# State-space heads: wrong-order token pairs zeroed by GpSimd behind the exponential, instead of masks added on TensorE

## The chip, the cores and the metric

The kernel runs on one core of one Trainium2 chip. The metric is the device time of one execution in microseconds (us). The kernel before takes 971.55 us, the median of three runs (970.40 to 972.12). One more execution was taken with the hardware profiler; it took 970.61 us, of which 968.5 us lie between the core's first and last instruction (the span).

The engines are named as in the profile: PE is TensorE's matmul side and PEld its weight load, DVE is VectorE, ACT is ScalarE, POOL is GpSimd, SP is the queue that issues the DMAs.

## The reference, cut to what matters

The program is one step of a small two-layer backbone. Layer 0 mixes by Fourier and attention, layer 1 by two recurrences side by side, one of them a bidirectional state-space model with 16 heads. Every layer is followed by a SwiGLU FFN. There are 128 context tokens and 256 latent tokens, worked on as three chunks of 128. The change is in the state-space heads, inside a chunk:

```
acs    = cumsum(dt * A)                        # per head and direction
diff   = acs[q] - acs[k]                       # 128 x 128 pairs of tokens
causal = tril(ones(Q, Q))                      # only k not after q
decay  = exp(where(causal, diff, -inf))        # wrong order: 0
y_diag = sum_k (C[q].B[k]) * decay[q,k] * dt[k] * x[k]
```

The backward direction does the same on the flipped sequence, so there the pairs on the other side of the diagonal count.

## The kernel before, in words

All activations lie with channels on the 128 partitions and tokens along the free dimension (384 tokens, or 386 columns with two extra columns for the modulation's shift). Every projection multiplies fp32 weights as a high and a low fp32r part: three matmuls of 386 columns for each 128x128 block of weights (`mm3`). The weights come in as chunks of eight blocks (`wr`); ACT writes the high part (`wh`) and DVE the low part (`wl`) of each chunk. These two steps run through the whole program and feed PE.

`Kernel.record` writes all operations into a recorder, and `Recorder.schedule` then sets the order of every engine's instructions by a list scheduler with a fixed cost for each operation: at each step it takes the operation that can start first by its costs. Within an engine the instructions then run strictly in that order. A changed operation or cost can therefore move any instruction behind it.

`odd_mixer` is layer 1's mixer. Its input projection yields 27 tiles; as each leaves PE, its own work on ACT and DVE follows: convolutions and SiLU (`cv`, `ct`), gates and scans of the RG-LRU (`lru`, `lru_scan`), and for every second `xs` tile two calls of `ssd`, each for two heads. So there are four groups of four heads. For each head `ssd` (line 1408) does the following:

- It builds `diff + log dt` for both directions in PSUM. One matmul `own x mv` (128x128 by 128x384) adds row and column terms; `own` and `mv` hold 112 used rows of 128, picked by the selector table `selv`.
- A second matmul into the same bank, `identr x mask` (line 1424), adds -2^100 to each pair in the wrong order. `mask` is made once in `deltas` from two triangular constants by two DVE instructions; `identr` is a rounded identity that ACT writes at the program's start.
- ACT takes the exponential out of PSUM into a tile `M` (128x384), one for each direction.
- DVE adds the two `M` tiles and multiplies by `cb` (the products C.B of the group).
- PE multiplies `M` with the tokens `xt`, together with the part of the carried state (`exs x Hc`), and DVE makes `ysum` of it.

POOL does nothing in this program but small memsets.

Of the kernel before, what the change touches and what calls it, by code (L numbers as in the profile page):

```python
# [101 lines left out]
def selectors():  # L102

    s = np.zeros((18, 128, NC_), np.float32)
    for h in range(16):
        for c in range(3):
            s[h, [c * 16 + h, 64 + c * 16 + h], c * 128:(c + 1) * 128] = 1.0
    for d in range(2):  # L110
        s[16 + d, [48 + d, 50 + d], 0:128] = 1.0
    return s


# [76 lines left out]
def R(v):  # L191
    return v.resolve() if isinstance(v, Vw) else v
# [279 lines left out]
class Kernel:  # L472
# [112 lines left out]
    def memset(self, out, v, eng="POOL"):  # L585
# [3 lines left out]
        else:  # L589
            self.rec.add("POOL", 0.1 + out.free / 900, [out], [], lambda: nc.gpsimd.memset(R(out), v))  # L590

    def dma(self, out, in_):
        nc = self.nc
        v = out if isinstance(out, Vw) else in_
        self.rec.add("SP", v.shape[0] * v.free * 4 / 400e3, [out], [in_], lambda: nc.sync.dma_start(R(out), R(in_)))  # L595
# [208 lines left out]
    def even_mixer(self):  # L804
# [216 lines left out]
        def pre(k):  # L1021
            if k == KC:
                return

            for j in ((0, 2) if k == 0 else (k + 2,) if k % 2 == 0 else ()):
                if j < KC:
                    if j:
                        self.ensure(-(-6 * j // NBLK), 0)
                    self.ada_pe(0, CM, j, 2)
                    self.gains(0, "norm_mix", j, j + 2)  # L1030
                    self.dma(self.x[:, j:j + 2, :], self.io["x"][:, j:j + 2, :])
                    self.ada_pe(0, SM, j, 2)
                    for i in (j, j + 1):
                        self.norm_xg(i)
                        self.shifts(0, SM, i)
                        self.norm_sq(i)
                    if j == 6:
                        self.dma(self.cons[:, NC00:NC0], self.io["consts"][:, NC00:NC0])
                        self.norm_close()
            if k == 6:  # L1040
                held.append(self.rec.ops[-1])
            if k == 7:
                self.early = self.EARLY
                self.rec.gate = held[0]
                load_consts("cos", "sin")
                pairs()
                self.rec.gate = None
            if k == 0:
                self.act(self.identr, self.ident, AF.Copy)

        self.dma(self.cons[:, CO["ident"]], self.io["consts"][:, CO["ident"]])
        self.norm_open()
# [69 lines left out]
    def odd_mixer(self):  # L1122
# [116 lines left out]
        def deltas(p):  # L1239

            t = self.slot("dtT")
            self.evac(t, p)
            for i in range(2):
                self.ts(t[:, SEG[i]], t[:, SEG[i]], t[:, 128 + i:129 + i], ALU.add)
            q = self.bank()
            for c in range(3):
                self.tp(q[:, c * 128:(c + 1) * 128], t[:, CH[c]:CH[c] + 128])
            v = self.tile("dv", 96, F32, "c")
            self.tt(v.split(3), q[:, 0:384].split(3)[:, :, 0:32], self.sm("dt_bias").unsqueeze(1).to_broadcast([128, 3, 32]), ALU.add)
            dt = self.tile("dt", 96, F32, "c")  # L1250
            self.softplus(dt, v, 96)
            dta = self.tile("dta", 96, F32, "c")
            d3 = dta.split(3)
            self.tt(d3, dt.split(3), negA.unsqueeze(1).to_broadcast([128, 3, 32]))
            q = self.bank()
            for c in range(3):
                self.mm(q[:, c * 32:c * 32 + 16], self.con("lo"), dta[:, c * 32:c * 32 + 16])
                self.mm(q[:, c * 32 + 16:c * 32 + 32], self.con("up"), dta[:, c * 32 + 16:c * 32 + 32])
            tot = self.bank()
            self.mm(tot[:, 0:96], self.ones, dta)  # L1260
            acs = self.tile("acs", 96, F32, "c")
            self.act(acs, q[:, 0:96], AF.Copy)
            de = self.tile("de", 96, F32, "c")
            self.tt(de, tot[:, 0:96], acs, ALU.subtract)
            self.act(de, de, AF.Exp)
            et = self.tile("et", 96, F32, "c")
            self.act(et, tot[:, 0:96], AF.Exp)
            q = self.bank()
            for c in range(3):
                self.tp(q[0:32, c * 128:(c + 1) * 128], acs[:, c * 32:(c + 1) * 32])  # L1270

            rr = self.slot("rr", NC_, F32R)
            self.act(rr[0:32], q[0:32, :NC_], AF.Copy)
            self.tt(rr[32:64], q[0:32, :NC_], rr[0:32].bitcast(F32), ALU.subtract)
            er = self.slot("er", NC_)
            self.act(er[0:32], q[0:32, :NC_], AF.Exp)
            ee = self.slot("ee", NC_, F32R)
            self.memset(ee[64:128].bitcast(F32), 0.0)
            self.split_hl(ee[0:32], ee[32:64], er[0:32])

            nacs = self.tile("nacs", 96, F32, "c")
            self.ts(nacs, dt, 2.0 ** -126, ALU.max)
            self.act(nacs, nacs, AF.Ln)
            steps = self.tile("steps", 96, F32, "c")
            q = self.bank()
            own = []
            for d in range(2):
                v = steps[:, d * 48:d * 48 + 48]
                ds = slice(d * 16, d * 16 + 16)
                self.tt(v.split(3), nacs.split(3)[:, :, ds], acs.split(3)[:, :, ds], ALU.subtract)  # L1290
                self.tp(q[0:48, d * 128:(d + 1) * 128], v)

                w, t = self.slot("ownt", 128), self.slot("own", 128, F32R)
                self.dma(w, self.io["selv"][16 + d, :, 0:128])
                self.act(t, w, AF.Copy)
                self.act(t[0:48], q[0:48, d * 128:(d + 1) * 128], AF.Copy)
                self.tt(t[64:112], q[0:48, d * 128:(d + 1) * 128], t[0:48].bitcast(F32), ALU.subtract)
                own.append(t)
            pick = self.slot("pick", 32)
            for z in range(2):  # L1300
                zs = slice(32 * z, 32 * z + 32)
                self.act(pick[zs], self.ident[zs, zs], AF.Copy)

            sel = [self.tile("sel", 1024, F32R, "k") for _ in range(2)]
            for z in range(2):
                self.memset(sel[z][64:128].bitcast(F32), 0.0)
                for d in range(2):
                    self.act(sel[z][0:64].split(8)[:, :, d * 64:d * 64 + 64],
                             pick[0:64, d * 16 + z * 8:d * 16 + z * 8 + 8].unsqueeze(2).to_broadcast([64, 8, 64]), AF.Copy)

            mask = []
            for mk in ("lo", "up"):
                t = self.slot("mask", NC_, F32R)
                self.ts(t.split(3), self.con(mk).unsqueeze(1).to_broadcast([128, 3, 128]), 2.0 ** 100, ALU.mult, -(2.0 ** 100), ALU.add)
                mask.append(t)
            dd = self.tile("dd", 96, F32, "c")
            self.tt(dd, dt, de)
            S.update(dd=dd, own=own, et=et, rr=rr, ee=ee, sel=sel, mask=mask)

        def bc(i, p):  # L1320
            y = conv(p, self.sm("csw")[:, (8 + i) * 4:(8 + i) * 4 + 4], self.sm("csb")[:, 8 + i:9 + i])
# [86 lines left out]
        def ssd(j):  # L1408
# [4 lines left out]
            for hb in range(2):  # L1413
                h = 2 * j + hb
                q = [self.bank() for _ in range(2)]

                t, mv = self.slot("mvt", NC_), self.slot("mv", NC_, F32R)
                self.dma(t, self.io["selv"][h])
                self.dma(t[48:52], S["rr"].bitcast(F32)[h:64:16])
                self.act(mv, t, AF.Copy)  # L1420
                for d in range(2):
                    self.mm(q[d][:, :NC_], S["own"][d], mv, True, False)
                for d in range(2):
                    self.mm(q[d][:, :NC_], self.identr, S["mask"][d], False, True)
                    m = self.slot("M", NC_)
                    self.act(m, q[d][:, :NC_], AF.Exp)
                    M[hb, d] = m
                self.tt(M[hb, 0], M[hb, 0], M[hb, 1], ALU.add)
                self.tt(M[hb, 0], M[hb, 0], S["cb"][g])
                q = self.bank()  # L1430
                self.mm(q[:, 0:256], S["sel"][h // 8][:, h % 8 * 128:h % 8 * 128 + 128], S["ee"][:, 128:384])
                ex[hb] = self.slot("exs", NS_)
                self.tt(ex[hb], q[:, 0:256], S["cs"][g])
# [113 lines left out]
    def record(self, n_chunks):  # L1547
# [8 lines left out]
        self.memset(self.scT, 0.0)  # L1556
        self.mod = [Tl(f"mod{l}", None, (128, 48, 2), F32).view() for l in range(2)]
        self.G = Tl("G", None, (128, KC, 2), F32).view()
        self.identr = self.tile("identr", 128, F32R)
        self.ident = self.con("ident")  # L1560
        self.ones = self.con("ones")
        self.act(self.scT[:, :, 0:2], self.sm("condT").split(8), AF.Silu)
# [166 lines left out]
```

## Time and profile before

| what | value |
|---|---|
| median of three runs | 971.55 us |
| profiled execution, and its span | 970.61 us, 968.5 us |
| PE busy | 946.1 us, 98% of the span |
| DVE busy | 730.9 us, 75% |
| ACT busy | 498.1 us, 51% |
| POOL busy | 6.5 us, 1% |
| granted TensorE clock, mean | 0.998 |

Matmuls are pipelined and the profile models their ends, so PE's busy share says that it had work and not that it ran at its peak; how long a matmul occupies PE is read from the distance of two starts. The shares of DVE and ACT are means over stages: in layer 1's mixer (about 430 to 640 us) both are far higher than over the whole program.

### The profile page before, as it was taken

The page shows a single profiled execution, that of the slowest core. Times are in us where ns is not written, and L with a number is a line of the kernel's source. Part 1 is how long each engine was busy: PE and PEld are TensorE (multiplying, and loading weights), DVE is VectorE, ACT ScalarE, POOL GpSimd, SP SyncE. Part 2 cuts the span into 40 slices and gives each one's busy share as a digit, 9 for nine tenths or more (in the row PEclk, how much of TensorE's full clock was granted, in tenths as well). Part 3 has the DMA queues.
Part 4 walks back from the last instruction along what each step waited for, and adds up shares of the span by engine and source line. Part 5 has one row for each costly group of instructions (what it writes and reads, how often), then busy time and mean ns, then how long its engine had stood idle before and what let it go on. Part 6 is the DMA issues. An engine that isn't in the chain of part 4 may idle for free.

```text
span 968.5 us, 16058 instructions
## 1 busy us (share of the span) xinstructions
PE 946.1 (98%) x6093; PEld 908.5 (94%) x6093; DVE 730.9 (75%) x1552; ACT 498.1 (51%) x958; POOL 6.5 (1%) x44
## 2 busy tenths in 40 slices
PE   6999999999999999999999999999999999999998
PEld 4987879999999999999989799999999999999998
DVE  3588774999999999996689798996888555553332
ACT  4569774534433443244488899854454334332220
POOL 0000000000000000000000000000000000000000
PEclk9999999999999999999999999999999999999999
DMA  9983523874666666755432321234733333333440
GB/s 357 365 323 107 196 88 110 300 243 156 219 227 206 229 220 227 248 183 188 143 118 98 126 72 66 93 108 135 288 124 129 128 115 129 131 120 120 150 139 17
DMA packets 49900, 163.23 MB, mean 169 GB/s; under 512 B 5728, under 2 KB 11936, under 8 KB 49824
## 3 DMA queue, kind: packets, MB, share of 16 engines
q1 hardware_dynamic: 49824, 162.22, 48.1%
q8 instruction: 48, 0.79, 0.3%
q14 instruction: 28, 0.23, 0.1%
HBM read 159.72 MB, written 2.37 MB: 167 GB/s over the span
## 4 chain that ended last, share of the span: by engine, by line
PE 86%; ACT 5%; DVE 5%; DMA 2%; issue 1%; SPq 0%; DVEq 0%; ACTq 0%
PE ps L602 84%; DMA ar<-in_ada 2%; PE ps L606 2%; DVE cv L565 1%; DVE wl L552 1%; ACT kk L542 1%; DVE ly L571 1%; ACT wh L542 1%; SPq L595 0%; ACT ex L542 0%; ACT L542 0%; ACT kl L542 0%; ACT t L542 0%; ACT cv L542 0%; ACT M L542 0%
## 5 line engine op out<-in xcount | busy, mean ns | idle before, releaser
L542 ACT ACTIVATE wh<-wr 128x1024 fp32r<-128x1024 f32 x191 | 202.0, 1058 | 346.3 <-PE ps L602 226.1
L602 PE MATMUL ps<-xh,wh 128*128 128x386 f32 x1016 | 347.3, 343 | 1.8 <-ACT rstd L542 1.5
L602 PE MATMUL ps<-xl,wh 128*128 128x386 f32 x1016 | 346.9, 341 | 0.0
L602 PE MATMUL ps<-xh,wl 128*128 128x386 f32 x1016 | 345.8, 340 | 0.0
L552 DVE TENSOR_TENSOR wl<-wr,wh 128x1024 fp32r<-128x1024 f32 x191 | 233.2, 1221 | 98.0 <-ACT wh L542 94.5
L602 PEld LDWEIGHTS ps<-xh,wh 128*128 128x128 f32 x1016 | 191.9, 189 | 5.2 <-ACT rstd L542 1.9
L602 PEld LDWEIGHTS ps<-xl,wh 128*128 128x128 f32 x1016 | 192.3, 189 | 2.1 <-issue 1.5
L602 PEld LDWEIGHTS ps<-xh,wl 128*128 128x128 f32 x1016 | 192.5, 189 | 0.7 <-issue 0.2
L565 DVE SCALAR_TENSOR_TENSOR junk<-ar,scb 128x1024 bf16<-128x1024 f32 x112 | 136.5, 1219 | 3.1 <-DMA ar<-in_ada 2.6
L602 PE MATMUL ps<-gl,wh 128*128 128x384 f32 x352 | 118.7, 337 | 0.0
L602 PE MATMUL ps<-gh,wl 128*128 128x384 f32 x352 | 118.6, 337 | 0.0
L602 PE MATMUL ps<-gh,wh 128*128 128x384 f32 x352 | 118.6, 337 | 0.0
L552 DVE TENSOR_TENSOR ft<-ps,rstd 128x386 f32<-128x386 f32 x88 | 48.2, 557 | 53.0 <-PE ps L602 50.8
L602 PEld LDWEIGHTS ps<-gl,wh 128*128 128x128 f32 x352 | 66.1, 188 | 0.0
L602 PEld LDWEIGHTS ps<-gh,wh 128*128 128x128 f32 x352 | 66.1, 188 | 0.0
L602 PEld LDWEIGHTS ps<-gh,wl 128*128 128x128 f32 x352 | 66.1, 188 | 0.0
L602 PE MATMUL ps<-ml,wh 128*128 128x384 f32 x160 | 54.2, 339 | 0.6 <-DVE ml L552 0.6
L602 PE MATMUL ps<-mh,wl 128*128 128x384 f32 x160 | 54.0, 338 | 0.0
L602 PE MATMUL ps<-mh,wh 128*128 128x384 f32 x160 | 52.7, 339 | 1.1 <-ACT mh L542 1.1
L542 ACT ACTIVATE xh<-x,G 128x128 fp32r<-128x128 f32 x64 | 26.3, 445 | 23.4 <-DVE x L565 16.6
L542 ACT ACTIVATE gh<-fs 128x384 fp32r<-128x384 f32 x44 | 23.1, 525 | 25.8 <-DVE fs L565 25.6
L565 DVE SCALAR_TENSOR_TENSOR fs<-ft,fs 128x128 f32<-128x128 f32 x88 | 33.3, 414 | 3.7
(229 smaller groups left out, 1016.0 us busy)
## 6 DMA issues: line engine op xcount, KB each, us to landing
wr<-in_wst SPq DMA_DIRECT2D x191, 512.0 KB
ar<-in_ada SPq DMA_DIRECT2D x96, 512.0 KB
mvt<-in_selv SPq DMA_DIRECT2D x16, 192.0 KB
x<-in_x SPq DMA_DIRECT2D x4, 386.0 KB
out_y<-x SPq DMA_DIRECT2D x8, 193.0 KB
scb<-in_cond SPq DMA_DIRECT2D x2, 512.0 KB
lw<-in_lru_w SPq DMA_DIRECT2D x2, 512.0 KB
Hc<-in_h SPq DMA_DIRECT2D x2, 256.0 KB
```

Source lines behind the costliest of these rows:

```text
L542: lambda: nc.scalar.activation(out=R(out), in_=R(in_), func=func, bias=R(bias), scale=R(scale), accum_out=R(accum_out)),
L552: self.dve(out, [a, b], out.free, lambda: nc.vector.tensor_tensor(out=R(out), in0=R(a), in1=R(b), op=op))
L565: lambda: nc.vector.scalar_tensor_tensor(out=R(out), in0=R(a), scalar=R(s), in1=R(b), op0=op0, op1=op1, accum_out=R(accum_out)),
L571: lambda: nc.vector.tensor_tensor_scan(out=R(out), data0=R(a), data1=R(b), initial=R(initial), op0=ALU.mult, op1=ALU.add))
L602: self.rec.add("PE", c / 1e3, [out], [lhsT, rhs], lambda: nc.tensor.matmul(R(out), R(lhsT), R(rhs), start=start, stop=stop), cols=cols)
L606: self.rec.add("PE", 0.109, [out], [in_, ident], lambda: nc.tensor.transpose(R(out), R(in_), R(ident)), cols=2 * in_.shape[0])
```

## The change

Three things change together.

- The matmul `identr x mask` is gone for all 16 heads and both directions, and with it `mask`, `identr` and the instructions that make them.
- Behind each exponential stands a new POOL instruction, `affine_select`, which reads and writes the 128x384 tile `M` in place and puts 0 where the pair is in the wrong order (`causal`). DVE's add of the two tiles now waits for POOL instead of ACT.
- The selector table uses 26 rows that were zero before: the 128 tokens are put into blocks of five, and the matmul `own x mv` itself adds -2^100 to pairs in the wrong order that lie in different blocks. Number and size of these matmuls stay as they are; only the table's values differ.

```diff
@@ selectors()
+    t = np.arange(128)
+    for b, r in enumerate([*range(52, 64), *range(112, 126)]):
+        s[:16, r] = np.tile(t // 5 == b, 3)
+        s[16, r, 0:128] = np.where(t // 5 > b, -(2.0 ** 100), 0.0)
+        s[17, r, 0:128] = np.where(t // 5 < b, -(2.0 ** 100), 0.0)
@@ class Kernel
+    def causal(self, v, d):
+        nc = self.nc
+        s = 1 if d == 0 else -1
+        self.rec.add("POOL", 0.14 + v.free / 1200, [v], [v],
+                     lambda: nc.gpsimd.affine_select(out=R(v.split(3)), in_=R(v.split(3)), compare_op=ALU.is_ge, fill=0.0, base=0,
+                                                     pattern=[[0, 3], [s, 128]], channel_multiplier=-s))
@@ even_mixer
-            if k == 0:
-                self.act(self.identr, self.ident, AF.Copy)
@@ deltas
-            mask = []
-            for mk in ("lo", "up"):
-                t = self.slot("mask", NC_, F32R)
-                self.ts(t.split(3), self.con(mk).unsqueeze(1).to_broadcast([128, 3, 128]), 2.0 ** 100, ALU.mult, -(2.0 ** 100), ALU.add)
-                mask.append(t)
@@ ssd
-                    self.mm(q[d][:, :NC_], S["own"][d], mv, True, False)
+                    self.mm(q[d][:, :NC_], S["own"][d], mv)
                 for d in range(2):
-                    self.mm(q[d][:, :NC_], self.identr, S["mask"][d], False, True)
                     m = self.slot("M", NC_)
                     self.act(m, q[d][:, :NC_], AF.Exp)
+                    self.causal(m, d)
                     M[hb, d] = m
@@ record
-        self.identr = self.tile("identr", 128, F32R)
```

On PE, in the second group of heads (`own x mv` makes the pair terms, `sel x ee` the factor for the carried state), the kernel before issues for two heads:

```order
L602 MATMUL ps_6085<-mv_5932,own_5240 128x384
L602 MATMUL ps_6089<-mv_5932,own_5247 128x384
L602 MATMUL ps_6085<-mask_5212,identr_71 128x384
L602 MATMUL ps_6089<-mask_5242,identr_71 128x384
L602 MATMUL ps_6095<-ee_5024,sel_4962 128x256
L602 MATMUL ps_6102<-mv_5940,own_5240 128x384
L602 MATMUL ps_6104<-mv_5940,own_5247 128x384
L602 MATMUL ps_6102<-mask_5212,identr_71 128x384
L602 MATMUL ps_6104<-mask_5242,identr_71 128x384
L602 MATMUL ps_6114<-ee_5024,sel_4962 128x256
```

The changed kernel issues for two heads at the same place:

```order
L617 MATMUL ps_6065<-mv_5956,own_5236 128x384
L617 MATMUL ps_6071<-mv_5956,own_5241 128x384
L617 MATMUL ps_6074<-ee_5022,sel_4960 128x256
L617 MATMUL ps_6080<-mv_5962,own_5236 128x384
L617 MATMUL ps_6090<-mv_5962,own_5241 128x384
L617 MATMUL ps_6098<-ee_5022,sel_4960 128x256
```

The two mask matmuls of each head are gone and what stood around them has closed up. Over the whole program PE has 32 matmuls less.

On POOL, in the stretch in which the first group of heads comes, the kernel before has only memsets of the convolution's edge columns (`X`):

```order
L590 MEMSET X_5280 128x2
L590 MEMSET X_5283 128x2
L590 MEMSET X_5949 128x1
L590 MEMSET X_5949 128x2
L590 MEMSET X_6007 128x1
```

The changed kernel has there, behind one instruction without operands (ISA):

```order
L597 MEMSET X_5269 128x2
L597 MEMSET X_5274 128x2
L604 ISA
L604 AFFINE_SELECT M_5831<-M_5831 128x384
L604 AFFINE_SELECT M_5838<-M_5838 128x384
L604 AFFINE_SELECT M_5846<-M_5846 128x384
L604 AFFINE_SELECT M_5852<-M_5852 128x384
L604 AFFINE_SELECT M_5857<-M_5857 128x384
L604 AFFINE_SELECT M_5864<-M_5864 128x384
L604 AFFINE_SELECT M_5918<-M_5918 128x384
L604 AFFINE_SELECT M_5922<-M_5922 128x384
L597 MEMSET X_5942 128x1
```

All eight selects of a group stand one behind the other, each waiting for its exponential.

On DVE, in the fourth group (`M,M` is the add of the two directions, `M,cb` the product, `wl` a weight chunk's low part, `xw` and `exs` operands of later matmuls), the kernel before has:

```order
L552 TENSOR_TENSOR M_6880<-M_6880,M_6885 128x384
L552 TENSOR_TENSOR xw_6952<-xt_6939,dd_5729 128x128
L552 TENSOR_TENSOR xw_6957<-xt_6939,dd_5729 128x128
L552 TENSOR_TENSOR M_6880<-M_6880,cb_5651 128x384
L552 TENSOR_TENSOR M_6890<-M_6890,M_6894 128x384
L552 TENSOR_TENSOR xw_6952<-xt_6963,dd_5729 128x128
L552 TENSOR_TENSOR xw_6957<-xt_6963,dd_5729 128x128
L552 TENSOR_TENSOR M_6890<-M_6890,cb_5651 128x384
L552 TENSOR_TENSOR M_6910<-M_6910,M_6915 128x384
L552 TENSOR_TENSOR exs_6989<-ps_6866,cs_5622 128x256
L552 TENSOR_TENSOR M_6910<-M_6910,cb_5651 128x384
L552 TENSOR_TENSOR wl_6998<-wr_6600,wh_6926 128x1024
```

The changed kernel has:

```order
L559 TENSOR_TENSOR M_6870<-M_6870,M_6874 128x384
L559 TENSOR_TENSOR M_6884<-M_6884,M_6892 128x384
L559 TENSOR_TENSOR xw_6929<-xt_6943,dd_5723 128x128
L559 TENSOR_TENSOR xw_6936<-xt_6943,dd_5723 128x128
L559 TENSOR_TENSOR M_6870<-M_6870,cb_5645 128x384
L559 TENSOR_TENSOR M_6884<-M_6884,cb_5645 128x384
L559 TENSOR_TENSOR M_6897<-M_6897,M_6903 128x384
L559 TENSOR_TENSOR exs_6973<-ps_6859,cs_5616 128x256
L559 TENSOR_TENSOR M_6897<-M_6897,cb_5645 128x384
L559 TENSOR_TENSOR wl_6980<-wr_6596,wh_6961 128x1024
```

DVE has the same work, and an add that now waits for two selects has the same followers queued behind it, among them the next `wl`.

Outside layer 1's mixer the order changes only in single places at the program's start. On ACT two table loads fall away, one at the start (beside `identr`) and one in the mixer.

## Rows read from the trace of the kernel before

**Rows 1.** Page, busy time and share of the span of each engine.
```profile
PE 946.1 (98%) x6093; PEld 908.5 (94%) x6093; DVE 730.9 (75%) x1552; ACT 498.1 (51%) x958; POOL 6.5 (1%) x44
```

**Rows 2.** Busy time by stretch: length, PE, PEld, DVE, ACT, POOL, clock, DMA.
```profile
500.00:640.00 140.00, 135.60 (x850) 123.21 (x851) 127.62 (x298) 120.87 (x252) 0.78 (x11) 1.00 0.29 98
```

**Rows 3.** Chain of waits, longest pieces: start, us, engine, tile, line, instructions.
```profile
5.38 9.23 DMA ar<-in_ada
...
213.53 266.31 PE ps L602 x1520
...
509.44 12.11 PE ps L602 x81
...
532.26 11.04 PE ps L602 x73
543.33 0.59 ACT th L542
...
559.37 30.13 PE ps L602 x185
...
638.52 74.14 PE ps L602 x425
```

**Rows 4.** Same table by stretch: groups one and four of heads, and behind.
```profile
507.00:523.00 16.00, 15.95 (x110) 14.87 (x111) 15.19 (x34) 13.54 (x34) 0.54 (x8) 1.00 0.42 136
...
589.00:602.00 13.00, 12.71 (x75) 12.08 (x74) 12.72 (x29) 12.92 (x30) 0.00 (x0) 1.00 0.23 82
...
602.00:638.50 36.50, 34.85 (x219) 32.02 (x217) 36.03 (x90) 29.53 (x55) 0.10 (x1) 1.00 0.31 105
```

**Rows 5.** The tile `mask`: its matmuls, ns min/median/max, first and last start.
```profile
L602 PE MATMUL ps<-mask,identr x32: 334/338/341, 505.3 to 590.9; 128*128 128x384 f32 x32
```

**Rows 6.** Timeline of PE, mask matmuls: start, us, line, tiles, count.
```profile
507.35 0.34 PE L602 MATMUL ps<-mask,identr 128*128 128x384 f32 x1
...
526.90 0.51 PE L602 MATMUL ps<-mask,identr 128*128 128x384 f32 x2
...
556.28 0.34 PE L602 MATMUL ps<-mask,identr 128*128 128x384 f32 x1
...
588.04 0.51 PE L602 MATMUL ps<-mask,identr 128*128 128x384 f32 x2
...
588.86 0.51 PE L602 MATMUL ps<-mask,identr 128*128 128x384 f32 x2
```

**Rows 7.** What PE waited for, 500 to 560 us: total, times, longest.
```profile
PE ps L602 <- DVE exs L552: 1.7, 2, 1.5
```

**Rows 8.** Groups by line: ACT's table loads, then POOL's memsets.
```profile
L542 ACT ACT_TABLE_LOAD x18 | 23.1, 1283 | 1.0 <-PEq L1644 0.7
...
L590 POOL MEMSET sel<- 64x1024 f32 x2 | 1.9, 950 | 330.2 <-DVE junk L565 330.2
...
L590 POOL MEMSET ee<- 64x384 f32 x1 | 0.4, 416 | 0.1
```

**Rows 9.** Timeline of ACT, DVE and PE: the first group's way through `M`.
```profile
507.12 2.36 ACT L542 ACTIVATE M<-ps 128x384 f32<-128x384 f32 x6
...
515.08 0.56 DVE L552 TENSOR_TENSOR M<-M,cb 128x384 f32<-128x384 f32 x1
...
518.03 1.04 PE L602 MATMUL ps<-M,xt 128*64 128x128 f32 x16
```

**Rows 10.** Timeline of POOL, before and at the first group; then DVE.
```profile
434.67 0.95 POOL L590 MEMSET sel<- 64x1024 f32 x1 [3.77 <-DVE junk L565]
...
454.81 0.35 POOL L590 MEMSET X<- 128x1 f32 x4 [0.21 <-PE ps L602]
509.81 0.14 POOL L590 MEMSET X<- 128x1 f32 x2 [54.65 <-DVE M L552]
...
434.48 1.22 DVE L552 TENSOR_TENSOR wl<-wr,wh 128x1024 fp32r<-128x1024 f32 x1
...
438.36 1.22 DVE L552 TENSOR_TENSOR wl<-wr,wh 128x1024 fp32r<-128x1024 f32 x1
```

More of the change, by code (lines that the diff above doesn't have):

```diff
@@ L1309, in deltas @@
                              pick[0:64, d * 16 + z * 8:d * 16 + z * 8 + 8].unsqueeze(2).to_broadcast([64, 8, 64]), AF.Copy)
-            mask = []
-            for mk in ("lo", "up"):
-                t = self.slot("mask", NC_, F32R)
-                self.ts(t.split(3), self.con(mk).unsqueeze(1).to_broadcast([128, 3, 128]), 2.0 ** 100, ALU.mult, -(2.0 ** 100), ALU.add)
-                mask.append(t)
             dd = self.tile("dd", 96, F32, "c")
             self.tt(dd, dt, de)
-            S.update(dd=dd, own=own, et=et, rr=rr, ee=ee, sel=sel, mask=mask)
+            S.update(dd=dd, own=own, et=et, rr=rr, ee=ee, sel=sel)
         def bc(i, p):
```

## Prediction

> **What bounds the kernel now.** I read the page's busy shares first, then the chain of waits, then busy times by stretch, and at the places of the change the timelines. PE has work for 98% of the span, DVE for 75%, ACT for 51% and POOL for 1% [rows 1]. The chain shows where this mean hides something: before about 505 us and behind 638.5 us it runs over PE almost alone (1520 matmuls in one piece of 266.31 us, later 425 in 74.14 us), so there PE's matmuls set the time, and nothing of the change lies there [rows 3]. The piece of 266.31 us also gives the price of a matmul: 266.31 / 1520 = 0.175 us from start to start. The 338 ns that the tile's row shows are the modelled, overlapping length [rows 5].
>
> The change lies in layer 1's mixer. From 500 to 640 us PE is busy for 135.6 of 140 us, DVE for 127.6 and ACT for 120.9 [rows 2]. Three engines are close to full, and the chain goes from one to another: PE from 507 to 543 us, ACT and DVE to 556, PE from 559.4 to 589.5, then ACT, and from about 606 to 638.5 DVE [rows 3]. The table by stretch shows how little room is left on DVE where the selects come: 15.19 of 16 us in the first group of heads, 12.72 of 13 in the fourth, and 36.03 of 36.5 behind it [rows 4].
>
> **The change part by part.** *The mask matmuls.* 32 are gone [rows 5], 32 x 0.175 = 5.6 us of PE time. Only those count that lie where PE is the chain. Of the first two groups these are the 12 from 507.35 to 526.90 us (the first and the last of them stand in the rows; four start earlier, while the chain is on DVE). In the third group PE waits for DVE (1.7 us in two waits, on `exs`) [rows 7]; a shorter queue in front of that wait saves nothing, and only the one at 556.28, behind it, counts. In the fourth group four start before the chain leaves PE at 589.5: two at 588.04 and two at 588.86 [rows 6]. 12 + 1 + 4 = 17, and 17 x 0.175 = 3.0 us.
>
> *The masks, `identr` and table loads.* The two DVE instructions that make `mask` run some 50 us before the first head, on an engine that is not in the chain there: nothing. `identr` and its table load at the start stand in front of the first matmul's operand on ACT, but PE starts when the first `ar` chunk lands, and the chain there is a DMA piece of 9.23 us [rows 3]: nothing. One table load less in the mixer is 1.28 us of ACT [rows 8]. I count it at zero, since the chain leaves ACT for DVE between 547 and 556 us and behind 605; at most it brings its 1.28 us.
>
> *The selects.* 32 instructions on an engine that does nothing but memsets and idles 54.65 us before the first group [rows 10]. The instruction without operands in front of them stands behind a memset that ends at 455.2 us, more than 50 us before the first exponential, which covers it. The trace has no select; the nearest rows are POOL's memsets: 0.416 us for 384 columns and 0.950 for 1024 [rows 8], which is 0.83 ns a column on 0.10 us fixed. A select reads and writes. If both overlap it costs like the memset, 0.42 us; if they take turns, 0.10 + 2 x 0.32 = 0.74. I take 0.45, close to the row. The exponentials come every 0.39 us (six in 2.36) [rows 9], so POOL falls behind by at most 6 x 0.06 = 0.4 us.
>
> *The wait moved from ACT to POOL.* Behind DVE's add of two `M` tiles stand its product, `xw`, `exs` and the next `wl`, and PE waits for `wl`. In the first group the last product starts at 515.08 and ends at 515.64, and PE takes up `M,xt` at 518.03: 2.4 us of room [rows 9]. PE comes 8 x 0.175 = 1.4 us earlier now, so 1.0 us is left, and a select with its hand-over (0.45 and some 0.15) fits in. In the later groups the room is several us. Nothing, as long as a select only adds its own length to this way.
>
> *Sum.* 970.61 - 3.0 = 967.6 us for an execution like the profiled one. The median lies 0.94 us above that execution, so 968.5 us.
>
> *What speaks against it.* DVE and POOL may get in each other's way. The only row that can show it is a 950 ns memset of POOL from 434.67 us, which lies inside a `wl` of DVE from 434.48: that `wl` takes 1.22 us, and so does the one from 438.36, which has no memset beside it [rows 10]. So a POOL instruction that writes costs DVE nothing here; one that reads is nowhere in the trace. The Trainium skill (SBUF — State Buffer, section Who interferes with whom) says that a DVE instruction with two SBUF inputs contends with a GpSimd instruction that reads SBUF, not with one that only writes it, and that the loser blocks for the whole instruction. With the half that the memset shows the trace agrees; by the other half rival 2 would hold.
>
> **The rivals.** Let T be what DVE loses for each select. In the first group DVE has 16 - 15.19 = 0.8 us of idle time, so its last product is 8T - 0.8 later, and PE, with 1.0 us of room, stands for 8T - 1.8. In the fourth group 0.3 us is free and nothing worth naming behind it (0.47 us in 36.5) [rows 4], so 8T - 0.3 goes straight to the end, because DVE's work behind the fourth group is what the mixer ends with. With the 3.0 us from above the whole is 16T - 5.1 us, where both waits are real (T over 0.23). Groups two and three have idle DVE time behind them and give back what they lose.
>
> *Rival 1, the saving is met by the other engines.* T is 0.2 to 0.4 us, or T is zero and DVE, with under half a us idle in the last 36.5, simply doesn't finish earlier. For it: DVE's rows. Against it: the chain enters the fourth group from PE, so what PE saves before 589.5 also lets ACT and DVE begin earlier. Time: -1.9 to +1.3 us, about 970.6 as profiled, 971.5 as a median.
>
> *Rival 2, DVE stops while POOL reads.* Place: DVE beside the selects, PE at the first `M,xt`, and the end of the mixer. For it: nearly all that DVE does there (`wl`, `cv`, `M,M`, `M,cb`, `xw`) has both inputs in SBUF, and DVE has no spare time. Against it: some of its work there (`exs`, `X`, `ysum`) takes one input from PSUM, the memset's row shows no hindrance, and DVE's own waits leave holes. Price: with T = 0.45, 16 x 0.45 - 5.1 = +2.1 us, 972.7 as profiled and 973.7 as a median; with T = 0.74 it is +6.7 and 978.3. It decides from T = 0.44 us on.
>
> *Rival 3, the change doesn't do what it says.* The order shows 32 matmuls less and 32 selects more; this I leave at no chance.
>
> **How the numbers follow.** A measurement of this kernel can tell 0.2%, 1.9 us, from no change. Forecast (T near zero): 0.43, with a range of its own from 964.7 (all 5.6 us and the table load, -6.9) to 969.6 us. Rival 1: 0.23. Rival 2: 0.34. The predicted time is the forecast's, 968.5 us. The range reaches from 965.5, short of the forecast's best, to 977.0, short of rival 2's dearest select: the two ends left out hold some 2 in 10. Faster by over 0.2%: 0.43; within: 0.23; slower: 0.34.
>
> **What would show it.** Right: in the changed kernel's profile 32 fewer matmuls, PE's stretch from 507 us reaches the `th` of ACT some 2 us earlier, the mixer ends about 3 us earlier; `wl` and `M,M` keep their lengths (1.22 and 0.55 us) beside selects; a select takes 0.4 to 0.5 us from start to start. Wrong: `wl`, `cv` or `M,M` show longer forms in the four groups, DVE waits for POOL before `M,M`, PE waits for `M` in front of `M,xt`, or the last `wl` of the mixer ends later than before. If selects take 0.74 us or more, DVE's wait for them alone would cost the gain.

## The result: half a per cent slower, and the profile after

The changed kernel takes 976.45 us (median of 5 runs, 975.77 to 976.88), the kernel before 971.55 us in the same comparison (5 runs, 970.40 to 972.42). The ratio is 1.0051, with a 95% interval from 1.0038 to 1.0064. The profiled execution has a span of 974.7 us against 968.5 us, 6.2 us more; the medians differ by 4.9 us, and the profiled execution before was one of its faster ones. The forecast was 968.5 us and faster; the time lies inside the range, on the other side of no change, and only because the range was stretched to hold rival 2.

The page of the changed kernel, busy time and share of the span by engine, answers to [rows 1]:

```profile
PE 947.4 (97%) x6061; PEld 907.7 (93%) x6061; DVE 736.9 (76%) x1550; ACT 496.2 (51%) x955; POOL 29.4 (3%) x76
```

The change did what it says: 32 matmuls less (6093 to 6061) and 32 instructions more on POOL (44 to 76). But PE is busy 1.3 us longer with 32 matmuls less, and DVE 6.0 us longer with two instructions less. Both must do the same work more slowly somewhere.

Where that is, the busy times by stretch tell (length, PE, PEld, DVE, ACT, POOL, clock, DMA). The first row answers to [rows 2], the second to the first group in [rows 4]; the last runs to the end of the mixer's last `ml` made from `gu` on DVE (640.2 us before, 646.5 after):

```profile
500.00:640.00 140.00, 131.69 (x792) 116.85 (x792) 129.41 (x285) 117.46 (x246) 23.79 (x43) 0.96 0.28 92
507.00:523.00 16.00, 14.14 (x92) 12.84 (x90) 14.96 (x28) 12.70 (x30) 6.85 (x16) 1.00 0.38 122
524.00:540.00 16.00, 14.60 (x82) 13.20 (x77) 15.14 (x32) 9.87 (x27) 5.60 (x8) 0.89 0.13 38
594.00:607.00 13.00, 11.82 (x53) 11.17 (x54) 12.81 (x23) 12.10 (x28) 5.54 (x8) 0.74 0.12 40
500.00:646.50 146.50, 137.15 (x822) 121.99 (x821) 135.63 (x303) 120.83 (x252) 23.79 (x43) 0.97 0.28 93
```

Read the counts, not only the times. In the same 140 us DVE is busy for 129.4 us where it was 127.6, yet gets through 285 instructions where it got through 298. In the first group it is 28 in 16 us, before 34. PE's granted clock, 1.00 through the mixer before, has a mean of 0.89 and 0.74 in two stretches, so part of each ran at the lower level of 1.2 GHz.

DVE's groups by shape from 500 to 612 us name the instructions that grew (busy, mean ns | idle before them, and what ended it):

```profile
L572 DVE SCALAR_TENSOR_TENSOR cv<-X,smalls,cv 128x386 f32<-128x386 f32 x30 | 19.9, 676 | 1.9 <-ACT cv L549 1.7
...
L559 DVE TENSOR_TENSOR M<-M,M 128x384 f32<-128x384 f32 x16 | 10.4, 666 | 0.9 <-POOL M L604 0.9
L559 DVE TENSOR_TENSOR M<-M,cb 128x384 f32<-128x384 f32 x16 | 9.7, 619 | 0.0
L559 DVE TENSOR_TENSOR exs<-ps,cs 128x256 f32<-128x256 f32 x16 | 6.3, 416 | 0.1
L559 DVE TENSOR_TENSOR X<-ps,rstd 128x386 f32<-128x386 f32 x10 | 5.5, 555 | 0.4 <-PE ps L617 0.2
...
L559 DVE TENSOR_TENSOR xw<-xt,dd 128x128 f32<-128x128 f32 x16 | 4.9, 341 | 0.0
```

The same groups in the kernel before:

```profile
L565 DVE SCALAR_TENSOR_TENSOR cv<-X,smalls,cv 128x386 f32<-128x386 f32 x33 | 19.9, 614 | 2.0 <-ACT cv L542 1.6
...
L552 DVE TENSOR_TENSOR M<-M,M 128x384 f32<-128x384 f32 x16 | 8.6, 549 | 0.0
L552 DVE TENSOR_TENSOR M<-M,cb 128x384 f32<-128x384 f32 x16 | 8.6, 549 | 0.0
L552 DVE TENSOR_TENSOR exs<-ps,cs 128x256 f32<-128x256 f32 x16 | 6.4, 415 | 0.3 <-PE ps L602 0.3
...
L552 DVE TENSOR_TENSOR xw<-xt,dd 128x128 f32<-128x128 f32 x16 | 3.9, 283 | 0.6 <-ACT xt L542 0.6
```

Three of the `cv` now fall behind 612 us (33 before). `X` has a mean of 555 ns in both. The forms with two SBUF inputs (`cv`, `M,M`, `M,cb`, `xw`) are longer by 58 to 117 ns in the mean. `exs` and `X`, with one input from PSUM, keep their length to a nanosecond. And DVE hardly waits for POOL: 0.9 us in all, once, behind the first selects.

The tile `M` on POOL and DVE (ns min/median/max, first and last start) and PE's waits on `M` over the whole span (total, times, longest):

```profile
L604 POOL TENSOR_SCALAR_AFFINE_SELECT M<-M x32: 514/832/2003, 507.8 to 601.0; 128x384 f32<-128x384 f32 x32
L559 DVE TENSOR_TENSOR M<-M,M x16: 542/546/885, 510.3 to 605.5; 128x384 f32<-128x384 f32 x16
```

```profile
PE ps L617 <- ACT M L549: 3.2, 3, 2.5
PE ps L617 <- DVE M L559: 1.9, 1, 1.9
```

A select takes 0.51 us at best and 0.83 at the median: POOL stands too. The `M,M` has a median of 546 ns (549 before), so the growth is in a few long ones and not spread over all. Single rows of DVE show what happens, first beside the first select, then in the second group, where one select follows on another from 529.4 to 534.0 us:

```profile
508.19 1.22 DVE L559 TENSOR_TENSOR wl<-wr,wh 128x1024 fp32r<-128x1024 f32 x1
...
529.61 0.87 DVE L559 TENSOR_TENSOR M<-M,M 128x384 f32<-128x384 f32 x1
530.41 0.87 DVE L572 SCALAR_TENSOR_TENSOR cv<-X,smalls,cv 128x386 f32<-128x386 f32 x1
531.20 0.87 DVE L559 TENSOR_TENSOR M<-M,cb 128x384 f32<-128x384 f32 x1
```

The first select starts at 507.78 us, beside a `cv` and this `wl`, and is the one of 2.00 us; the `wl` keeps its 1.22. In the second group the two engines take turns: each of these DVE instructions takes 0.87 us where it took 0.55 to 0.61, one every 0.79 us, and the selects between them come every 0.79 us too, where two undisturbed ones (from 528.07 us, beside `exs`) start 0.47 us apart. So a DVE instruction that meets a select loses some 0.3 us, and the others keep their length.

The chain of waits (start, us, engine, tile, line, instructions) shows where this reaches the end; it answers to [rows 3]:

```profile
507.78 1.49 POOL M L604
...
510.29 0.85 DVE M L559
...
536.01 10.85 PE ps L617 x72
546.89 0.59 ACT th L549
...
594.19 4.42 DVE cv L572 x6
...
604.65 1.41 DVE M L559 x3
...
646.85 13.20 PE ps L617 x76
```

The chain reaches ACT's `th` at 546.89 us, before at 543.33: 3.6 us are lost over the first two groups. PE takes the chain over for good at 646.85 instead of 638.52. In the timeline of PE the first group reads so (start, us; what it waited for in brackets):

```profile
516.73 0.82 PE L617 MATMUL ps<-M,xt 128*64 128x128 f32 x10
...
519.41 0.62 PE L617 MATMUL ps<-M,xt 128*64 128x128 f32 x6 [1.86 <-DVE M L559]
...
595.17 0.58 PE L617 MATMUL ps<-ee,sel 128*128 128x256 f32 x1 [2.54 <-ACT M L549]
```

PE reaches `M,xt` at 516.73 us, 1.3 us earlier than before [rows 9]: the saving of eight matmuls arrives (1.4 us forecast). Then it stands 1.86 us for a later product of DVE, and in the fourth group 2.54 us for ACT's exponentials.

### The profile page after: what moved, and what is told of

Same layout as the page of the kernel before. It is cut to its first block, busy times and chain, and to the rows that moved or that the text cites. A ratio compares the mean times of both kernels' runs of the same rounds, so it can differ in the third digit from the quotient of the medians.

```text
span 974.7 us, 16021 instructions
## 1 busy us (share of the span) xinstructions
PE 947.4 (97%) x6061; PEld 907.7 (93%) x6061; DVE 736.9 (76%) x1550; ACT 496.2 (51%) x955; POOL 29.4 (3%) x76
## 4 chain that ended last, share of the span: by engine, by line
PE 80%; DVE 9%; ACT 5%; issue 4%; DMA 1%; SPq 0%; POOL 0%; DVEq 0%; POOLq 0%; ACTq 0%
PE ps L617 78%; DVE cv L572 2%; DVE wl L559 1%; PE ps L621 1%; DVE M L559 1%; DMA ar<-in_ada 1%; DVE ly L578 1%; ACT L549 1%; ACT kk L549 1%; ACT wh L549 1%; SPq L610 0%; ACT th L549 0%; ACT ex L549 0%; ACT t L549 0%; ACT kl L549 0%
```

## The experiments

Theories: L, POOL's *reading* slows DVE (as rival 2 has it); W, the *wait* moved behind POOL is what costs; O, the *order* of the instructions that the new program has is the worse one. Later came C, what PE saves comes back as waits and these bring its clock down, and D: every microsecond of DVE work in this stage is a microsecond of the time, whatever PE does. In the lines of code `...` marks what is left out. Between two changed kernels the differences below are those of their medians, good to about 0.7 us, since the kernel before had medians from 971.07 to 971.74 us beside these runs. Against the kernel before they are the ratio's share of 971.55 us.

**The wait, the write and the read, taken apart.** Three kernels keep the changed kernel's order and touch only the instruction on POOL. The first leaves it out:

```
-   lambda: nc.gpsimd.affine_select(out=R(v.split(3)), in_=R(v.split(3)), compare_op=ALU.is_ge, ...)
+   lambda: None)
```

> The changed kernel in its own order, with the 32 selects planned but not issued, so DVE's add waits for the exponential alone (pairs in the wrong order inside a block of five tokens are not zeroed). Theory L (DVE and POOL block each other): without selects the masks' saving is left, about 3 us under the kernel before, 967 to 970 us, no wl, cv or M,M longer than before, no half-speed stretch of the clock in the mixer. Rival O (the new order is at fault): still 974 to 977 us, with PE's wait of 2.5 us in the fourth group and the half-speed stretch behind it. Rival W (the longer way through M): 967 to 970 us as with L.

Measured: 970.16 us (969.14 to 972.49), ratio 0.9990 [0.9982, 0.9999]. That is at the upper edge of what L and W say and far from O. But L's mark that no half clock is left in the mixer fails: PE's wait in the fourth group and the half clock behind it, both named for O, are there without selects too (shown further below).

The second puts a memset of the same tile in its place, which writes and doesn't read; DVE waits for POOL as in the changed kernel:

```
+   lambda: nc.gpsimd.memset(R(v), 1.0))
```

> The changed kernel in its own order, each select replaced by a POOL memset of the same tile M: it writes the tile and DVE still waits for POOL, but nothing is read (M is overwritten, so the pair weights are left out). Theory L: DVE's instructions keep their lengths, memsets take 0.42 us, and the time is at most 1 us above the run without selects, 967 to 971 us. Rival W: most of the loss stays, since the wait and 0.42 of 0.5 us of its length stay: 973 to 976 us. Rival O: 974 to 977 us, as without selects.

Measured: 970.06 us (968.37 to 972.0), ratio 0.9985 [0.9976, 0.9994]. The third reads `M` but writes a tile that nobody reads, so that nothing waits for its result (DVE's add overwrites one of the two `M` tiles, so it still has to let the select read that one first):

```
+   lambda: nc.gpsimd.affine_select(out=R(self.scr.split(3)), in_=R(v.split(3)), compare_op=ALU.is_ge, ...)
+   self.scr = self.tile("scr", NC_, BF16)
```

> The changed kernel in its own order, each select reads M and writes a bf16 tile that nobody reads, so DVE's add does not wait for POOL (the pairs in the wrong order inside a block of five tokens are not zeroed). Theory L: wl, cv, M,M and M,cb still show longer forms, DVE loses some 7 us in the four groups, and the time lies 2 to 4 us above the run without selects, 970 to 973 us; what is left to the changed kernel is the wait. Rival W: like the run without selects, 967 to 970 us. Rival O: 974 to 977 us.

Measured: 975.98 us (975.30 to 976.48), ratio 1.0048 [1.0035, 1.0060]. L had left some 3 us to the wait and is missed by these; W is missed altogether, and O's range, which it meets, was ruled out by the first two.

So the 32 selects cost 976.45 - 970.16 = 6.3 us, 0.2 us each. A wait and a write alone cost nothing (-0.1 us); a read of `M` whose result nobody waits for costs 5.8. DVE's groups from 500 to 612 us show the same, first without selects:

```profile
L572 DVE SCALAR_TENSOR_TENSOR cv<-X,smalls,cv 128x386 f32<-128x386 f32 x33 | 20.0, 616 | 2.1 <-ACT cv L549 1.8
...
L559 DVE TENSOR_TENSOR M<-M,M 128x384 f32<-128x384 f32 x16 | 8.6, 551 | 0.0
```

then with the memset, first DVE's group and then POOL's own, from 500 to 640 us:

```profile
L559 DVE TENSOR_TENSOR M<-M,M 128x384 f32<-128x384 f32 x16 | 8.6, 551 | 0.0
...
L604 POOL MEMSET M<- 128x384 f32 x32 | 12.6, 420 | 126.4 <-ACT M L549 122.5 <-DMA wr<-in_wst 3.5 <-DVE M L559 0.4
```

then with the select that nobody waits for:

```profile
L572 DVE SCALAR_TENSOR_TENSOR cv<-X,smalls,cv 128x386 f32<-128x386 f32 x30 | 20.5, 695 | 1.9 <-ACT cv L549 1.8
...
L559 DVE TENSOR_TENSOR M<-M,M 128x384 f32<-128x384 f32 x16 | 10.5, 669 | 0.4 <-POOL scr L604 0.4
...
L559 DVE TENSOR_TENSOR exs<-ps,cs 128x256 f32<-128x256 f32 x16 | 6.3, 417 | 0.1
```

With the memset `M,M` keeps its 551 ns, with the reading select it takes 669, and the add waits 0.4 us for POOL there, before it may overwrite what is read; `exs` is the same in all (415 to 418 ns). How much DVE loses in all is in the row by stretch of the kernel without selects, up to its last `ml` made from `gu`; beside it stands a stretch that is used further below:

```profile
500.00:640.40 140.40, 134.74 (x823) 120.69 (x821) 128.72 (x304) 120.97 (x252) 0.78 (x11) 0.98 0.30 96
...
580.00:600.00 20.00, 17.36 (x82) 16.12 (x82) 17.00 (x38) 19.05 (x42) 0.00 (x0) 0.83 0.16 52
```

DVE does the same work in 128.72 us here and in 135.63 in the changed kernel: 6.9 us, or 0.22 us for each select in the mean. That is a little more than the 6.3 us of time.

The Trainium skill (SBUF — State Buffer, section Who interferes with whom) names just this pair: a DVE instruction with two SBUF inputs against a GpSimd instruction that reads SBUF, not against one that only writes it. The traces agree (669 against 551 ns). Its rule that the contention is an exclusive lock fits the single rows shown with the profile after: the engines take turns, and the first select stands for a whole `wl`. But DVE stands for some 0.3 us and not for the 0.47 that a select takes from start to start. The 0.22 us are less because they are a mean: not every select meets a DVE instruction with two SBUF inputs.

**Twice the dose.** The changed kernel with a second select behind each, that reads the tile again and writes aside:

```
+   lambda: [nc.gpsimd.affine_select(out=R(o.split(3)), in_=R(v.split(3)), ...) for o in (v, self.scr)])
```

> The changed kernel in its own order, with a second select behind each one that reads the result again and writes a bf16 tile that nobody reads (64 instead of 32 selects, values unchanged). Theory L: another 5 to 6 us, 981 to 984 us, and DVE's forms longer twice as often. Rival (DVE meets only a limited number of them, or the cost is the first select's wait): 976 to 978.5 us.

Measured: 988.1 us (986.41 to 990.26), ratio 1.0169 [1.0149, 1.0188]: the second 32 selects cost 11.7 us where the first cost 6.3, more than L's 5 to 6. DVE's groups, 500 to 612 us:

```profile
L559 DVE TENSOR_TENSOR M<-M,cb 128x384 f32<-128x384 f32 x13 | 9.4, 736 | 0.0
...
L559 DVE TENSOR_TENSOR M<-M,M 128x384 f32<-128x384 f32 x13 | 8.2, 628 | 7.5 <-POOL M L604 7.5
```

Here the wait, which was free, costs too: with 64 selects POOL can't keep up, and DVE waits 7.5 us for it. The loss grows with the dose, as reading requires, but not in a straight line.

**Does the order matter?** The order of before with the mask matmuls planned but not issued:

```
-   self.mm(q[d][:, :NC_], self.identr, S["mask"][d], False, True)
+   self.mm(q[d][:, :NC_], self.identr, S["mask"][d], False, True, issue=False)
```

> The kernel before in its own order with the 32 mask matmuls planned but not issued, and the selector table of the changed kernel; no selects (pairs in the wrong order inside a block of five tokens are not zeroed). It prices the masks' removal by itself. All theories: 3.0 us less than before by the 17 matmuls on the chain, 967 to 970 us; if less than 1 us comes of it, ACT and DVE are what ends the mixer and the forecast's gain was never there. Against the run without selects it shows what the new order alone is worth: within 1 us by theory L, 5 us or more by O.

Measured: 974.27 us (971.27 to 975.35), ratio 1.0026 [1.0016, 1.0037], where every theory had 967 to 970. And the same with the 32 selects issued behind the exponentials:

```
-   self.act(m, q[d][:, :NC_], AF.Exp)
+   self.act(m, q[d][:, :NC_], AF.Exp, after=d)
+   # in act, behind nc.scalar.activation(...):
+   None if after is None else self.causal(out, after)
```

> The kernel before in its own order, mask matmuls planned but not issued, selector table of the changed kernel, and the 32 selects issued behind their exponentials: the whole change without its new order. Theory L (what costs is POOL reading beside DVE): 5 to 6 us over the run in the old order without selects, 978 to 981 us. Rival (the new order makes the selects dear): within 2 us of that run, 973 to 976 us.

Measured: 978.14 us (977.47 to 979.07), ratio 1.0066 [1.0051, 1.0081]. The new order is not to blame: with selects the old one is 1.7 us slower than the new one, and without them 4.1 us. The selects cost something in either: 978.14 - 974.27 = 3.9 us here, less than L's 5 to 6 and more than the rival's 2. But there was a surprise: 32 matmuls less, nothing in their place, and the kernel is 0.0026 x 971.55 = 2.5 us slower than before.

**Why less work was slower.** In that kernel's trace (its profiled execution took 972.71 us, one of its faster ones) the busy times by stretch, and PE's timeline:

```profile
540.00:560.00 20.00, 17.96 (x107) 14.08 (x106) 14.97 (x31) 17.38 (x33) 0.14 (x2) 0.87 0.36 123
560.00:580.00 20.00, 20.00 (x117) 18.12 (x116) 17.79 (x41) 17.56 (x39) 0.00 (x0) 0.96 0.19 60
```

```profile
555.23 0.69 PE L607 MATMUL ps<-mv,own 128*128 128x384 f32 x1 [1.55 <-DVE exs L557]
...
557.41 0.53 PE L607 MATMUL ps<-xl,wh 128*128 128x386 f32 x1
```

After a wait of 1.55 us for `exs` in the third group the clock of PE is at 1.2 GHz for the matmuls from there to about 562 us: a 128x386 matmul takes 0.53 us. PE is busy to the full from 560 to 580 us, so the loss isn't made up. The test issues the eight mask matmuls of this third group alone, with 24 of 32 still left out:

```
+   self.mm(q[d][:, :NC_], self.identr, S["mask"][d], False, True, issue=j in (4, 5))
```

> As the run in the old order with no mask matmul and no select, but with the 8 mask matmuls of the third group issued, where PE waits for DVE anyway (pairs in the wrong order inside a block of five tokens are not zeroed in the other groups). Theory C (the saved PE time comes back as PE waits, and these take TensorE's clock to half speed): no half-speed stretch of 6.83 us at 555 us, 968 to 970.5 us, so eight matmuls more make it 4 us faster. Rival (ACT and DVE end the mixer there, the clock is a by-product): 973 to 975 us, as without them.

Measured: 971.04 us (969.44 to 973.37), ratio 0.9994 [0.9984, 1.0005]. By stretch, and in PE's timeline:

```profile
540.00:560.00 20.00, 18.27 (x124) 15.38 (x121) 15.66 (x37) 18.95 (x40) 0.14 (x2) 1.00 0.33 104
```

```profile
554.08 0.44 PE L607 MATMUL ps<-mv,own 128*128 128x384 f32 x1 [1.48 <-DVE exs L557]
554.36 0.33 PE L607 MATMUL ps<-mask,identr 128*128 128x384 f32 x1
...
556.07 0.35 PE L607 MATMUL ps<-xl,wh 128*128 128x386 f32 x1
```

Eight matmuls *more*, and the kernel is 3.2 us faster, just short of what C says. The wait for `exs` is the same (1.48 us), the clock stays at 2.4 GHz here, and the 128x386 matmul takes 0.35 us. That the clock is the way by which the eight matmuls help is likely, but not shown. The two profiled executions also differ where nothing was edited: from 80 to 100 us the mean clock is 0.91 without the eight and 1.00 with them, and from 580 to 600 us it is 1.00 and 0.91. And the last kernel of this section, which has all 32 mask matmuls and the same wait of 1.48 us, still fell to 1.2 GHz behind it in its profiled execution:

```profile
540.00:560.00 20.00, 18.28 (x115) 14.97 (x114) 14.56 (x30) 17.53 (x33) 0.14 (x2) 0.93 0.35 120
```

```profile
557.30 0.52 PE L602 MATMUL ps<-xl,wh 128*128 128x386 f32 x1
```

The kernel without selects in the new order has a slow stretch too, in the fourth group (0.83 in its row by stretch above), where PE's timeline shows a wait for ACT as long as the changed kernel's:

```profile
589.96 0.58 PE L616 MATMUL ps<-ee,sel 128*128 128x256 f32 x1 [2.56 <-ACT M L549]
```

There the wait was filled with 16 matmuls by a tile of zeros:

```
+   [nc.tensor.matmul(R(o), R(self.zr), R(rhs), start=False, stop=z == 1) for z in range(2) for o in more]
```

> As the run of the changed kernel's order without selects, plus 16 matmuls of the mask's size in the fourth group that add zeros to the banks of the pair terms, 2.8 us of PE work in front of and inside PE's wait of 2.56 us there (pairs in the wrong order inside a block of five tokens are not zeroed). Theory C: the clock stays at full speed behind the wait, 966 to 968.5 us, 2 to 3 us faster than without the 16. Rival (ACT's late exponentials end it, not the clock): 970 to 971 us.

Measured: 969.93 us (969.24 to 970.96), ratio 0.9984 [0.9974, 0.9993]. By stretch:

```profile
580.00:600.00 20.00, 18.58 (x105) 17.46 (x104) 16.89 (x37) 19.11 (x41) 0.00 (x0) 1.00 0.16 52
```

The clock is whole, and the time is the same (969.93 against 970.16): in the fourth group ACT is busy for 19.1 of 20 us in both, and PE is not what is waited for. So half clock cost nothing here, and C is missed in this place. And with the clock kept, the new order without selects is only 1.6 us faster than before: the 3.0 us of the forecast were never there.

**Which groups pay?** Selects in the second and third group alone, then in the first and fourth alone; the others are planned and not issued:

```
+   self.causal(m, d, j in (2, 3, 4, 5))
```

> The changed kernel in its own order, with the selects of the second and third group of heads alone; those of the first and fourth are planned and not issued (there, pairs in the wrong order inside a block of five tokens are not zeroed). Theory D (DVE's work sets the mixer's length, so every microsecond that it loses counts, in whichever group): half of the 6.3 us that all 32 cost, about 973.3 us. Rival (the prediction's step that groups two and three give back what they lose): 970 to 971 us, as without selects.

Measured: 972.16 us (970.75 to 974.05), ratio 1.0009 [1.0000, 1.0018].

```
+   self.causal(m, d, j in (0, 1, 6, 7))
```

> The complement: the selects of the first and fourth group alone. Theory D: the other half, about 973.3 us. Rival (groups one and four carry it all): 975.5 to 976.5 us, like the changed kernel.

Measured: 974.67 us (973.86 to 975.28), ratio 1.0036 [1.0023, 1.0049]. Over the kernel without selects that is 2.0 and 4.5 us; the sum, 6.5, is the 6.3 of all 32. The groups add up, and the second and third give back a part, not the whole: both times lie between D's and the rival's.

**Is it DVE alone that counts?** The 16 products `M,cb` are left out on DVE, some 8 us of its time, in the new order without selects:

```
+   self.tt(M[hb, 0], M[hb, 0], S["cb"][g], issue=False)
```

> The changed kernel's order without selects, and DVE's 16 products of M with cb planned and not issued (left out: the weights C.B and the zeroing inside blocks), 16 x 0.47 = 7.5 us less DVE work, nothing else moved. Theory D: 963 to 966 us, most of the 7.5 us under the 970.2 us of the run that has the products. Rival P (PE's queue of matmuls sets the mixer's length): 968.5 to 970.5 us.

Measured: 967.97 us (967.53 to 968.71), ratio 0.9968 [0.9957, 0.9980], 2.2 us less than with the products and between D and P. The same edit in the kernel before, whose masks stay on PE:

> The kernel before, masks and all, with DVE's 16 products of M with cb planned and not issued (the weights C.B are left out). It asks the same of the kernel before, whose PE has 32 matmuls more. Theory D: 964 to 967 us against 971.3. Rival P: 970 to 971.5 us; then PE was the bound before, and the masks' removal should have shown.

Measured: 970.53 us (969.14 to 971.87), ratio 0.9993 [0.9984, 1.0002], in P's range and not clear of no change. Its busy times from 500 to 640 us and one group of DVE:

```profile
500.00:640.00 140.00, 135.74 (x843) 123.23 (x842) 119.43 (x270) 120.56 (x251) 0.78 (x11) 0.99 0.29 95
```

```profile
L552 DVE TENSOR_TENSOR xw<-xt,dd 128x128 f32<-128x128 f32 x16 | 3.9, 287 | 4.6 <-ACT xt L542 4.6
```

DVE has 8.2 us less to do than before (119.43 against 127.62 in [rows 2]) and the time falls by only 0.7 us: DVE now waits 4.6 us for ACT's `xt` in front of `xw`, where it waited 0.6. So D holds in one direction only. Work *added* to DVE (the selects' 6.9 us) costs almost its whole length in the new order and 3.9 of 5.4 us in the old; work *taken* from it is met by ACT and PE. Relief of PE alone gave 1.0 us in the new order (ratio 0.9990) and a loss in the old, of DVE alone 0.7 (0.9993), of both 3.1 (0.9968).

## Why the prediction was wrong

*The contention, costed at nothing.* This is the step that turned the sign. The forecast took T, what DVE loses for a select, near zero, because a memset inside a `wl` cost that `wl` nothing [rows 10]. The row was read rightly, but it shows a POOL instruction that writes, and the changed kernel with memsets shows that writes indeed cost nothing. It could not speak for a read, as the prediction itself said; then the forecast should not have rested on it. Measured: T = 0.22 us in the mean, some 0.3 where the two engines meet, and 6.3 us of time.

*Rival 2, right in mechanism, wrong in size.* DVE does stop, at the place named, in the forms named, and the mixer ends later. But its formula, 16T - 5.1, counts only two groups of four and takes the matmuls' full saving; it decides from T = 0.44 us. With the measured 0.22 it would give -1.5 us (under 0.23 us the first wait isn't real, so only 8T - 3.3 is left; rival 1's -1.9 at T = 0.2 should have been -1.7). Two of its steps failed: "Groups two and three have idle DVE time behind them and give back what they lose" (they pay 2.0 of the 6.3 us), and the saving.

*"17 x 0.175 = 3.0 us."* Mis-sized: 1.0 us without selects in the new order, and a loss of 2.5 us in the old. The chain of before was rightly read as being on PE there, but a chain shows one execution's latest arrivals, not how close behind the others are. PE came 1.3 us earlier to `M,xt` and then stood; in the fourth group it stood 2.5 us for the exponentials of ACT, with selects and without. [Rows 2] and [rows 4] had said it: three engines at 86 to 97% of the stretch. Rival 1, that the saving is met by the other engines, was right about this half.

*"The wait moved: nothing."* Right as put: with memsets, where DVE's `M,M` depends on POOL just as it does in the changed kernel, it stands for 0.0 us and the time is unchanged. "As long as a select only adds its own length" was the condition, and the selects, stretched to 0.83 us by DVE, broke it a little (0.9 us of waiting). The hand-over, put at some 0.15 us without a row, is smaller: with memsets the first exponential ends at 508.84 us and POOL starts at 508.90.

*A select at 0.45 us.* Right for an undisturbed one: two in a row start 0.47 us apart, though one is 0.51 long. Beside DVE they start 0.79 apart, above the range of 0.42 to 0.74, which was made from rows of memsets that nothing held up.

*Masks, `identr`, table load at zero.* Nothing in the runs speaks against it: the new order without selects has all of these edits and gains 1.0 us in all. These edits were not measured apart from the masks' removal.

Open are three things. First the clock's share: the changed kernel has more of its mixer at 1.2 GHz than the one without selects (a mean of 0.97 against 0.98). As far as a mean over the whole execution can tell it is the smaller share: at a mean clock of 0.992 the changed kernel took 976.45 and 976.47 us and the one without selects 970.87 to 972.49, so 4.0 to 5.6 of the 6.3 us are left. Second, why the second 32 selects cost nearly twice the first, beyond the 7.5 us of waiting. Third, by what way the eight matmuls of the third group save 3.2 us. That a lower clock and a longer time go together shows in the kernel before as well (27 executions beside the first four experiments: a median of 970.1 us with a mean clock of 0.998 or more, of 971.9 with 0.996), but not which brings the other.

## What to carry to other kernels

Work that is moved to POOL is free only as far as it does not read SBUF beside a DVE that is busy with two SBUF inputs; look at what POOL's instruction reads, and at DVE's busy share in that stage, before its own length. Where three engines are each close to full, taking work from one gained little here (0.7 to 1.0 us for 5.6 to 8.2 us of work, and a loss of 2.5 us in the old order), while adding to one cost most of it, so the chain of waits is no price list for such a stage. A row of before that can't show the disputed case is no reason to put its cost at zero.

## What the runs showed of the hardware

- A read by POOL slows DVE's forms with two SBUF inputs and is slowed by them: `M,M` from 551 to 666 ns in the mean and `cv` from 616 to 676, a select from 514 ns at best to 832 at the median, up to 2003. Where they meet they take turns: DVE instructions of 0.87 us instead of 0.55, one every 0.79 us. A memset at the same place takes 420 ns and slows nothing.
- Taking matmuls out can make a kernel slower, and putting some back faster: without its 32 mask matmuls the kernel before became 2.5 us slower (974.27 us), and with the eight around a wait of 1.5 us it was back at 971.04. The granted clock behind that wait was lower without the eight (0.87 against 1.00 in the same 20 us of the two profiles); that it is the cause is not shown. Where PE wasn't what was waited for, a half clock cost nothing (970.16 and 969.93 us).
